# One transformer layer on one core: the column widths of the products in three projection halves

## The chip, the core and the metric

The kernel runs on one core of a Trainium2 chip. The metric is the device time of one execution in microseconds (us), the median over the runs shown. A core has a matrix engine (TensorE, called PE in the profile, with its weight loads shown apart as PEld), a vector engine (DVE), a scalar engine (ACT), a third elementwise engine (POOL) and a queue engine (SP) that starts most transfers from memory.

## The reference

One layer works on 256 tokens of width 2048, in float32. It is a gated linear attention with its own projections, then a squared-ReLU MLP, with an RMSNorm before each and one at the end:

```
proj = rmsnorm(x, gla_norm) @ w_in            # q, k, v, r and a narrow gate
o    = linear attention over chunks of 64 tokens, from q, k, v and the gate
o    = rmsnorm(o, o_norm) * silu(r)
h    = x + o @ w_out
a    = relu(rmsnorm(h, mlp_norm) @ w_up)
out  = rmsnorm(h + (a * a) @ w_down, final_norm)
```

The change touches the two halves of the projection that makes r (2048 by 2048) and the first half of the projection by w_out (2048 by 2048).

## The kernel before

**Number format.** Every large product is made with operands in the format `F32R`, a shortened float32. To get the digits back, each operand is split in two: a high part, made by an ACT copy into `F32R` (line 127, in the profile `hi<-raw`), and a low part, made by a DVE subtraction of the high part (line 131, `lo<-raw,hi`). A product is then the sum of three: high by high, high by low and low by high. The profile shows the matmul's operands as plain `f32` in either format; which format it is follows from the tiles. Plain float32 products are used in a few places, among them the attention scores (line 518, `qt` and `kab`) and the transposes by the identity (line 592).

**A projection half.** `natural` (line 178) computes 256 tokens by 1024 output columns. The tokens are two groups `t` of 128, the 1024 columns are two accumulator banks of 512 (`HALF`), so four banks of PSUM hold the half. The 2048 inner elements are sixteen steps of 128. For each step, `weights` (line 144) allots one of five pairs of weight slots (`wpool`, tags `hi` and `lo`), starts the transfer of 128 by 1024 weights on SP's queue (line 168) and splits them. Then for each `t`, each of the three terms and each bank, `halves` (line 171) issues the products: the stationary operand is 128 by 128 of the activations, the moving operand is the weights. So a step has 2 x 3 x 2 = 12 pairs of stationary operand and bank.

**halves before.** A call covers one bank's 512 columns of one term. It cuts them into pieces of `T` = 256 columns and issues one matmul for each piece:

```
        for c in range(0, n, T) if n % T == 0 else (0,):
            m = slice(c, c + T) if n % T == 0 else slice(0, n)
            nc.tensor.matmul(o[:, m], x, w[:, m], start=first and c == 0, stop=last, skip_group_check=True)
```

A step thus has 24 matmuls of 256 columns, and a half has 384. Every matmul has a weight load of its own in the trace, also where the matmul ahead of it has the same stationary operand. `halves` is also called by the attention (line 561) and by the end of the kernel (line 1089).

**The three halves.** Line 600 makes the first half of r, line 625 the second half, line 646 the first half of the projection by w_out. A fourth call of the same form (line 655) makes the second half of w_out. The sixteen steps take the inner blocks in an order that `even_at` writes out: in the first half step 4 is block 3, in the other two step 4 is block 6; steps 8, 12 and 14 are blocks 8, 12 and 14 in all three. In the second half, block 6 takes its first 128 tokens from a copy in another tile (`xe_gt`).

**Other work on TensorE.** Behind each step but the last, `pump` (line 96) issues one item of a list of side work, in program order among the matmuls: the attention of one head and one token group in the first half, groups of eight 128 by 128 transposes in the other two, at steps 1 and 3. ACT and DVE run ahead of TensorE on the weights as far as the five slots allow.

**The first stage.** The call at line 388 uses cuts of 512, 256 and 272 columns. At its start TensorE waits for the first weights.

Of the kernel before, what the change touches and what calls it, by code (L numbers as in the profile page):

```python
# [32 lines left out]
P = 128  # L33
T = 256
NT = T // P
D = 2048
KT = D // P
# [3 lines left out]
KEYW = HEADS * DK  # L41
# [5 lines left out]
G = 1024  # L47
# [13 lines left out]
EVEN = (5, 6)  # L61
# [7 lines left out]
def tile_gla_mlp(ctx, tc, x, xt, cols, w_vg, w_in, w_gate, w_out, w_up, w_down, final_norm, out):  # L69
    nc = tc.nc  # L70
# [14 lines left out]
    def acc_banks(n):  # L85
        acc_free.rotate(-n)
        return [psum_bank(acc_free[k - n]) for k in range(n)]

    def aux_bank():
        aux_free.rotate(-1)  # L90
        return psum_bank(aux_free[-1], "aux")
# [4 lines left out]
    def pump(n=1):  # L96

        with tc.issue_after(last_hi[0].ins), tc.issue_after(last_lo[0].ins):
            for _ in range(n):
                if side:  # L100
                    side.popleft()()

    def flush():
        while side:
            side.popleft()()
# [38 lines left out]
    def weights(src, n, pieces=None, room=None, gap=None):  # L144


        to = room or slots()
        raw = raw_tile()
        loads, pieces = pieces or ([(0, n)], [(0, n)])
        for s in (slice(*p) for p in loads):  # L150
            dst = raw[:, s]
            if len(src.shape) == 3:
                dst = dst.rearrange("p (i c) -> p i c", i=2)
                with ExitStack() as order:

                    if n_raw[0] == 7:
                        order.enter_context(tc.issue_after(last_load[0].ins))
                    last_load[0] = nc.sync.dma_start(out=dst, in_=src)
                between = SLOT - OFF - 2 * GT if gap else 0
                to = [a[:, OFF - between : OFF + 2 * GT + between].rearrange("p (i c) -> p i c", i=2)[:, :, between:] for a in to]  # L160
                copy_hi(to[0], dst)
                with ExitStack() as order:
                    if last_sum[0]:
                        order.enter_context(tc.issue_after(last_sum[0]))
                    last_lo[0] = nc.vector.tensor_tensor(to[1], dst, to[0].bitcast(F32), op=ALU.subtract)  # L165
                return to
            else:
                last_load[0] = nc.sync.dma_start(out=dst, in_=src[:, s])
        return parts(raw, n, to, pieces)

    def halves(o, x, w, first, last):

        n = w.shape[-1]
        for c in range(0, n, T) if n % T == 0 else (0,):
            m = slice(c, c + T) if n % T == 0 else slice(0, n)
            nc.tensor.matmul(o[:, m], x, w[:, m], start=first and c == 0, stop=last, skip_group_check=True)  # L176

    def natural(row, source, n, cuts, pumps=1, ahead=None, order=range(KT)):

        acc = acc_banks(NT * len(cuts))  # L180
        acc = [acc[t * len(cuts) : (t + 1) * len(cuts)] for t in range(NT)]
        for step, kt in enumerate(order):
            wh, wl = weights(source(kt), n, ahead and ahead(kt))
            terms = lambda t: [(row(kt, t)[x], (wh, wl)[y]) for x, y in ((0, 0), (0, 1), (1, 0))]
            if ahead and step == 0:
                for c, (lo, hi) in enumerate(cuts):
                    for i in (0, 2, 1):
                        for t in range(NT):
                            s, w = terms(t)[i]
                            halves(acc[t][c], s, w[:, lo:hi], i == 0, False)  # L190
            else:
                for t in range(NT):
                    for i, (s, w) in enumerate(terms(t)):
                        for c, (lo, hi) in enumerate(cuts):
                            halves(acc[t][c], s, w[:, lo:hi], step == 0 and i == 0, step == KT - 1 and i == 2)
            if step < KT - 1:
                pump(pumps)
        return acc
# [4 lines left out]
    def turned(row, w, c0, even=(0,), acc=None):  # L203

        acc = acc or acc_banks(GT // P // 2)
        for kp in range(KT // 2):
            wh, wl = pair_of(w, kp, c0, even)
            for i in range(2):
                kt = 2 * kp + i
                ah, al = row(kt)  # L210
                for j in range(GT // P):
                    s = slice(j * P, (j + 1) * P)
                    o = acc[j // 2][:, j % 2 * T : (j % 2 + 1) * T]
                    for n, (u, m) in enumerate(((wh, ah), (wh, al), (wl, ah))):

                        nc.tensor.matmul(  # L216
                            o, u[:, i, s], m, start=kt == 0 and n == 0 and j % 2 == 0,
                            stop=kt == KT - 1 and n == 2, skip_group_check=True,
                        )
                if kt < KT - 1:  # L220
                    pump()
        return acc

    HALF = [(0, 512), (512, 1024)]

    def even_at(a, b):

        order = [kt for kt in range(KT) if kt not in EVEN]
        order.insert(a, EVEN[0])
        order.insert(b, EVEN[1])  # L230
        return order

    def rows(w, c0, n=G, r0=0):
        return lambda kt: w[r0 + kt * P : r0 + (kt + 1) * P, c0 : c0 + n]
# [64 lines left out]
    cuts = [(0, 512), (512, 768), (768, WMAX)]  # L299
# [81 lines left out]
    def put_v(bank, n, t, c0):  # L381
# [4 lines left out]
        )  # L386

    acc = natural(plain_x, rows(w_vg, 0, WMAX), WMAX, cuts, ahead=input_tile)
    flush()
    wrap_input(1, 0, KT - CUT)  # L390
# [90 lines left out]
    for half in range(2):  # L481
        acc = turned(stream_x, w_in, KEYW + half * GT, even=(0,) if half else (2, 3), acc=None if half else [aux_bank(), aux_bank()])
# [18 lines left out]
    for half in range(2):  # L501
        acc = turned(stream_x, w_in, half * GT, even=())
# [39 lines left out]


    acc = natural(row_x, rows(w_in, 3 * KEYW), G, HALF, order=even_at(9, 11))
    flush()
    for t in range(NT):
# [6 lines left out]
    def attend(hd, t):  # L553
        o = aux_bank()
        blocks = [(0, 0)] if t == 0 else [(0, P), (1, T)]
        vs = slice(hd * DV, (hd + 1) * DV)
        n = 0
        for src, lo in blocks:
            a_h, a_l = (a[hd][:, lo : lo + P] for a in (ath, atl))
            for s, v in ((a_h, vh), (a_h, vl), (a_l, vh)):  # L560
                halves(o, s, v[:, src, vs], n == 0, n == 3 * len(blocks) - 1)
                n += 1
        ss = st.tile([P, 1], F32, tag="oss", name="oss")
        sq = tmp.tile([P, DV], F32, tag="t512", name="sq", bufs=1)
        nc.scalar.activation(sq, o, AF.Square, scale=r1k[:, t : t + 1], accum_out=ss)
        nc.vector.tensor_scalar(ss, ss, 1.0 / DV, EPS, op0=ALU.mult, op1=ALU.add)
        rs = st.tile([P, 1], F32, tag="ors", name="ors")
        rsqrt(rs, ss)
        nc.vector.tensor_scalar(on[:, t, vs], o, r1k[:, t : t + 1], rs, op0=ALU.mult, op1=ALU.mult)
# [16 lines left out]
    def turn(src, row, gain, q):  # L586
# [6 lines left out]
        for i in range(4):  # L593
# [3 lines left out]
            nc.scalar.activation(dh, s, AF.Copy, scale=gain(kt))  # L597
            nc.vector.scalar_tensor_tensor(dl, s, gain(kt), dh.bitcast(F32), op0=ALU.mult, op1=ALU.subtract)

    acc = natural(lambda kt, t: (plain_x if kt == EVEN[1] else row_x)(kt, t), rows(w_in, 4 * KEYW), G, HALF, order=even_at(0, 6))  # L600
    flush()
    gate_out(acc, 0)
    oth, otl = (big.tile([P, KT * T + 192], F32R, tag="B", name="ot" + i) for i in "hl")
# [17 lines left out]
    def turns(src, row, gain, q0):  # L621
        return [f for q in (q0, q0 + 1) for f in (nothing, lambda q=q: turn(src, row, gain, q))]

    side.extend(turns(on, turned_o, gain_o, 0))
    acc = natural(row_x, rows(w_in, 5 * KEYW), G, HALF, order=even_at(2, 4))
    flush()
    gate_out(acc, G)

# [14 lines left out]
                sq = tmp.tile([P, 512], F32, tag="t512", name="sq", bufs=1)  # L643
                nc.scalar.activation(sq, h[:, t, lo : lo + 512], AF.Square, accum_out=hs[:, t, lo // 512 : lo // 512 + 1])

    acc = natural(row_o, rows(w_out, 0), G, HALF, order=even_at(2, 4))
    flush()
    add_h(acc, 0)
    hth, htl = (big.tile([P, KT, T], F32R, tag="A" + i, name="h" + i, bufs=1) for i in "hl")
# [5 lines left out]
    acc = natural(row_o, rows(w_out, G), G, HALF, order=even_at(2, 4))  # L655
# [221 lines left out]
    cuts = [HALF, [(0, 512), (512, 768), (768, 1024)]]  # L877
    acc = [[], []]
# [214 lines left out]
    for kt in range(KL):  # L1093
        k = kt - KL + ROOM
        w = weights(rows(w_down, G, G, (ROUNDS - 1) * MR)(kt), G, room=k >= 0 and [room[:, i, k, :] for i in range(2)])
# [20 lines left out]
    for t in range(NT):  # L1116
        for c, (lo, hi) in enumerate(cuts[t]):
            for kt, w in held:
                last_step(kt, w, t, c)
            o = acc[t][c]  # L1120
# [9 lines left out]
            last = nc.vector.tensor_scalar(sf, fs[:, t, n_fs[t] - 1 : n_fs[t]], 1.0 / D, some, op0=ALU.mult, op1=ALU.add)  # L1130
# [5 lines left out]
        for on_act, lo, hi in ((0, 0, 256), (1, 1280, 1536), (0, 256, 768), (1, 1536, 2048), (0, 768, 1280)):  # L1136
            s = hf[:, t, lo:hi]
# [44 lines left out]
```

## Time and profile before

| What | Value |
|---|---|
| Median of the runs | 1048.57 us (1048.22 to 1048.91, 2 runs) |
| Span of the profiled execution, first to last instruction | 1046.7 us |
| First half of r on the span | 190.32 to 242.07 us |
| Second half of r | 242.07 to 287.50 us |
| First half of w_out | 287.50 to 332.93 us |
| TensorE busy, share of the span | 99% |
| DVE busy | 81% |
| ACT busy | 67% |
| Granted TensorE clock, mean | 0.998 |

The profiled execution's own time beside its span is the first row: the runs' median is 1.9 us longer than the span, which is the time ahead of the first instruction and behind the last. A row of the timeline gives the start in us from the span's beginning, the length in us of the merged instructions, the engine, the source line, the operation, the tiles written and read, the shape and the count. A row of the groups ends in the busy time and the mean of one instruction in ns. The length of a matmul in the trace holds the time in which it passes through the array, so consecutive matmuls overlap: what one costs in a stream is read from the distance between starts. A row of the table by stretches gives the stretch, its length, the busy time of each engine with its count of instructions, the granted clock, the busy share of the transfer engines and what they moved.

### The profile page before, as it was taken

The page shows a single profiled execution, that of the slowest core. Times are in us where ns is not written, and L with a number is a line of the kernel's source. Part 1 is how long each engine was busy: PE and PEld are TensorE (multiplying, and loading weights), DVE is VectorE, ACT ScalarE, POOL GpSimd, SP SyncE. Part 2 cuts the span into 40 slices and gives each one's busy share as a digit, 9 for nine tenths or more (in the row PEclk, how much of TensorE's full clock was granted, in tenths as well). Part 3 has the DMA queues.
Part 4 walks back from the last instruction along what each step waited for, and adds up shares of the span by engine and source line. Part 5 has one row for each costly group of instructions (what it writes and reads, how often), then busy time and mean ns, then how long its engine had stood idle before and what let it go on. Part 6 is the DMA issues. An engine that isn't in the chain of part 4 may idle for free. (4 is left out here: it accounts for less than half of the span.)

```text
span 1046.7 us, 23145 instructions
## 1 busy us (share of the span) xinstructions
PE 1038.2 (99%) x9094; PEld 1037.8 (99%) x9094; DVE 843.9 (81%) x1225; ACT 704.2 (67%) x1045; POOL 110.1 (11%) x151
## 2 busy tenths in 40 slices
PE   9999999999999999999999999999999999999997
PEld 9999999999999999999999999999999999999997
DVE  6668645656465566889999999999999999999887
ACT  6785444546455455678678678778778777777785
POOL 0000000010000001111121111121111111211100
PEclk9999999999999999999999999999999999999999
DMA  9957665556655676678888887888888888887772
GB/s 341 332 166 220 188 197 167 156 146 180 199 180 183 187 215 191 169 222 226 227 237 231 238 239 212 247 231 226 237 236 226 238 241 223 234 232 221 236 241 88
DMA packets 112718, 225.21 MB, mean 215 GB/s; under 512 B 10289, under 2 KB 25265, under 8 KB 112481
## 3 DMA queue, kind: packets, MB, share of 16 engines
q1 hardware_dynamic: 95808, 207.39, 64.1%
q0 software_dynamic: 16128, 14.69, 9.3%
q10 hardware_dynamic: 672, 1.66, 0.4%
q8 instruction: 71, 1.16, 0.4%
q14 instruction: 39, 0.31, 0.1%
HBM read 221.60 MB, written 2.10 MB: 214 GB/s over the span
## 5 line engine op out<-in xcount | busy, mean ns | idle before, releaser
L118 ACT CAST hi<-raw 128x768 fp32r<-128x768 f32 (+4 forms) x610 | 490.3, 846 | 281.5 <-PE acc L176 105.5
L131 DVE TENSOR_TENSOR lo<-raw,hi 128x768 fp32r<-128x768 f32 (+3 forms) x226 | 241.8, 1071 | 124.8 <-ACT hi L118 122.2
L720 PE MATMUL acc<-hi,act 128*128 128x256 f32 x1696 | 247.8, 276 | 0.0
L720 PE MATMUL up<-hh,hi 128*128 128x256 f32 x1024 | 238.9, 276 | 0.0
L720 PE MATMUL up<-hl,hi 128*128 128x256 f32 x1024 | 238.8, 276 | 0.0
L165 DVE TENSOR_TENSOR lo<-raw,hi 128x1024 fp32r<-128x1024 f32 x160 | 194.7, 1219 | 30.9 <-ACT hi L118 30.6
L720 PEld LDWEIGHTS acc<-hi,act 128*128 128x128 f32 x1696 | 217.7, 188 | 0.0
L720 PEld LDWEIGHTS up<-hh,hi 128*128 128x128 f32 x1024 | 192.3, 188 | 0.0
L720 PEld LDWEIGHTS up<-hl,hi 128*128 128x128 f32 x1024 | 192.3, 188 | 0.0
L935 POOL DMA_DIRECT2D raw<-in_w_down x112 | 98.4, 878 | 515.0 <-DMA raw<-in_w_down 235.0
L999 DVE TENSOR_TENSOR lo<-raw,hi 128x1024 fp32r<-128x1024 f32 x112 | 136.4, 1218 | 1.6 <-ACT hi L118 1.1
L720 PE MATMUL up<-hh,lo 128*128 128x256 f32 x1024 | 137.0, 276 | 0.0
L720 PE MATMUL acc<-lo,act 128*128 128x256 f32 x848 | 134.0, 276 | 0.0
L720 PEld LDWEIGHTS up<-hh,lo 128*128 128x128 f32 x1024 | 125.7, 188 | 0.0
L720 PEld LDWEIGHTS acc<-lo,act 128*128 128x128 f32 x848 | 113.4, 188 | 0.0
L176 PE MATMUL acc<-hi,xA 128*128 128x256 f32 (+1 forms) x728 | 102.6, 279 | 0.0
L176 PEld LDWEIGHTS acc<-hi,xA 128*128 128x128 f32 x728 | 92.6, 189 | 0.2 <-ACT hi L118 0.2
L176 PE MATMUL acc<-lo,xA 128*128 128x256 f32 (+1 forms) x364 | 57.5, 278 | 0.0
L958 DVE TENSOR_TENSOR raw<-raw 128x256 f32<-128x256 f32 x112 | 47.4, 423 | 2.9
L959 DVE TENSOR_TENSOR raw<-raw 128x256 f32<-128x256 f32 x112 | 47.4, 423 | 2.8
L216 PE MATMUL acc<-xA,hi 128*128 128x256 f32 x288 | 49.2, 276 | 0.0
L176 PEld LDWEIGHTS acc<-lo,xA 128*128 128x128 f32 x364 | 48.9, 188 | 0.0
(159 smaller groups left out, 1197.7 us busy)
## 6 DMA issues: line engine op xcount, KB each, us to landing
raw<-in_w_up SPq DMA_DIRECT2D x128, 512.0 KB, 4.4
raw<-in_w_down SPq DMA_DIRECT2D x224, 256.0 KB, 4.4
raw<-in_w_in SPq DMA_DIRECT2D x80, 512.0 KB, 3.7
raw<-in_w_out SPq DMA_DIRECT2D x32, 512.0 KB, 3.7
raw<-in_w_down POOLq DMA_DIRECT2D x112, 128.0 KB, 5.1
raw<-in_w_down SPq DMA_DIRECT2D x16, 512.0 KB, 4.8
raw<-in_w_vg SPq DMA_DIRECT2D x14, 520.0 KB, 9.1
h<-in_x SPq DMA_DIRECT2D x4, 512.0 KB, 7.5
```

Source lines behind the costliest of these rows:

```text
L118: last_hi[0] = nc.scalar.copy(to, raw)
L131: last_lo[0] = nc.vector.tensor_tensor(lo[:, s], raw[:, s], hi[:, s].bitcast(F32), op=ALU.subtract)
L165: last_lo[0] = nc.vector.tensor_tensor(to[1], dst, to[0].bitcast(F32), op=ALU.subtract)
L176: nc.tensor.matmul(o[:, m], x, w[:, m], start=first and c == 0, stop=last, skip_group_check=True)
L216: nc.tensor.matmul(o, u[:, i, s], m, start=kt == 0 and n == 0 and j % 2 == 0, stop=kt == KT - 1 and n == 2, skip_group_check=True,)
L720: newest[0] = nc.tensor.matmul(o, x, w, start=first, stop=last, skip_group_check=True).ins
L935: nc.gpsimd.dma_start(out=raw[:, :T], in_=src[:, 0, T:], accum_op=ALU.add)
L958: tt(u[:, 2], u[:, 0], u[:, 2], op=ALU.add)
L959: tt(u[:, 1], u[:, 2], u[:, 1], op=ALU.subtract)
L999: last_lo[0] = nc.vector.tensor_tensor(to[1][:, :G], u, to[0][:, :G].bitcast(F32), op=ALU.subtract)
```

## The change

`halves` gets a list of widths. Where a list is given, one call's 512 columns are cut by it; where none is given, the pieces are the ones of before. A table `WIDE` gives the list for four steps, and `natural` looks a step up in it. The three calls named above hand the table over; the fourth half and all other calls of `natural` and `halves` don't.

```diff
-    def halves(o, x, w, first, last):
+    def halves(o, x, w, first, last, widths=None):
 
         n = w.shape[-1]
-        for c in range(0, n, T) if n % T == 0 else (0,):
-            m = slice(c, c + T) if n % T == 0 else slice(0, n)
-            nc.tensor.matmul(o[:, m], x, w[:, m], start=first and c == 0, stop=last, skip_group_check=True)
-
-    def natural(row, source, n, cuts, pumps=1, ahead=None, order=range(KT)):
+        lo = 0
+        for d in widths or ([T] * (n // T) if n % T == 0 else [n]):
+            m = slice(lo, lo + d)
+            nc.tensor.matmul(o[:, m], x, w[:, m], start=first and lo == 0, stop=last, skip_group_check=True)
+            lo += d
+
+    WIDE = {4: [512], 8: [P] * 4, 12: [384, P], 14: [512]}
+
+    def natural(row, source, n, cuts, pumps=1, ahead=None, order=range(KT), wide={}):
...
-                            halves(acc[t][c], s, w[:, lo:hi], step == 0 and i == 0, step == KT - 1 and i == 2)
+                            halves(acc[t][c], s, w[:, lo:hi], step == 0 and i == 0, step == KT - 1 and i == 2, wide.get(step))
...
-    acc = natural(lambda kt, t: (plain_x if kt == EVEN[1] else row_x)(kt, t), rows(w_in, 4 * KEYW), G, HALF, order=even_at(0, 6))
+    acc = natural(lambda kt, t: (plain_x if kt == EVEN[1] else row_x)(kt, t), rows(w_in, 4 * KEYW), G, HALF, order=even_at(0, 6), wide=WIDE)
...
-    acc = natural(row_x, rows(w_in, 5 * KEYW), G, HALF, order=even_at(2, 4))
+    acc = natural(row_x, rows(w_in, 5 * KEYW), G, HALF, order=even_at(2, 4), wide=WIDE)
...
-    acc = natural(row_o, rows(w_out, 0), G, HALF, order=even_at(2, 4))
+    acc = natural(row_o, rows(w_out, 0), G, HALF, order=even_at(2, 4), wide=WIDE)
```

With `P` = 128, steps 4 and 14 have 12 matmuls of 512 columns instead of 24 of 256; step 8 has 48 of 128; step 12 has 12 of 384 and 12 of 128. Over the four steps that is 96 matmuls, as before. No transfer, split, wait or accumulator bank is moved.

## Prediction

> **What bounds the kernel now.** I read the page's head and its slices first, to see which engine sets the time, and then the table by stretches for the changed halves.
>
> ```profile
> span 1046.7 us, 23145 instructions
> PE 1038.2 (99%) x9094; PEld 1037.8 (99%) x9094; DVE 843.9 (81%) x1225; ACT 704.2 (67%) x1045; POOL 110.1 (11%) x151
> ```
>
> TensorE is busy for 99% of the span, and it has as many weight loads (PEld) as matmuls. The head alone doesn't prove that TensorE is the bound, since a matmul's length holds its passage through the array. The stretches do: here are four ordinary steps of the second half (its steps 8 to 11), then that whole half, then the first half of w_out.
>
> ```profile
> core 0: us, PE busy (x) PEld busy (x) DVE busy (x) ACT busy (x) POOL busy (x), PEclk, DMA share, GB/s
> 265.74:276.62 10.88, 10.88 (x99) 10.88 (x97) 4.90 (x4) 4.20 (x4) 0.00 (x0) 1.00 0.60 193
> 242.07:287.50 45.43, 45.43 (x403) 45.43 (x401) 25.55 (x29) 23.37 (x31) 0.00 (x0) 1.00 0.61 186
> 287.50:332.93 45.43, 45.43 (x403) 45.43 (x402) 25.29 (x29) 21.14 (x26) 0.00 (x0) 1.00 0.61 186
> ```
>
> Four steps are 96 matmuls (the other three counted are overlaps at the edges), so a 256-column product costs 10.88 / 96 = 0.1133 us from start to start, and a step of 24 costs 2.72 us. The clock is fully granted, and DVE and ACT are busy for about half of each stretch. Who waits in the two whole halves (242.07 to 332.93 us) is in the table of waits:
>
> ```profile
> ACT hi L118 <- PE acc L176: 40.5, 25, 1.7
> DVE lo L131 <- ACT hi L118: 37.3, 29, 1.5
> ```
>
> ACT, which splits the weights, waits 25 times for TensorE's products to free a slot, and no row has TensorE waiting. So in these halves a microsecond more on TensorE is a microsecond more in the end, and there is no idle time on TensorE that could hide it.
>
> **What sets the 0.1133 us.** A 256-column product is 256 columns of streaming and one weight load, and the load for the next product runs beside the streaming. Which of the two is longer decides what 128 columns cost. Between streaming products the trace can't separate them, but once, at the start of the first stage, TensorE ran dry and the load stands alone. Four timeline rows, each pair from narrow windows on weight loads and on matmuls:
>
> ```profile
> 8.87 0.30 PEld L176 LDWEIGHTS acc<-hi,xA 128*128 128x128 f32 x2 [0.25 <-ACT hi L118]
> 8.98 0.19 PEld L176 LDWEIGHTS acc<-hi,xA 128*128 128x128 f32 x1
> ...
> 8.87 0.39 PE L176 MATMUL acc<-hi,xA 128*128 128x256 f32 x1
> 9.10 0.40 PE L176 MATMUL acc<-hi,xA 128*128 128x272 f32 x2
> ```
>
> The load at 8.87 follows an idle wait. The matmul that needs it is noted at the same moment but is 0.39 us long, 0.11 more than the usual 276 ns: it stood waiting for its weights. The second load starts only at 8.98, 0.11 us after the first, and the second matmul at 9.10. I read this as: a load takes 0.11 us, and the next begins when the product ahead of it begins. Then no product, however narrow, can follow another in less than about 0.11 us.
>
> **What other widths cost.** No row has this format under 256 columns, and the only wider pieces, of 272, stand in the first stage. The nearest rows for the slope are the plain float32 products of the scores:
>
> ```profile
> 164.64 1.70 PE L518 MATMUL aux<-qt,kab 128*128 128x128 f32 x12
> 165.08 0.49 PE L518 MATMUL aux<-qt,kab 128*128 128x192 f32 x2
> 165.41 0.60 PE L518 MATMUL aux<-qt,kab 128*128 128x192 f32 x3
> ...
> L518 PE MATMUL aux<-qt,kab x48: 270/275/328, 164.6 to 187.4; 128*128 128x128 f32 x32, 128*128 128x192 f32 x16
> ```
>
> The first head's first four records are of 128 columns: 165.08 - 164.64 = 0.44, so 0.11 us each. The next two are of 192: 165.41 - 165.08 = 0.33, so 0.165 each. The extra 64 columns cost some 0.055 us, or 0.86 ns a column, about twice the 0.1133 / 256 = 0.44 ns of the changed format, and the code's 24 products are 48 records. So a plain float32 record passes its columns at half speed, and there are two of them for a product. A 192-column record streams like 384 columns of our format: 0.165 us, which is my price for 384. For 512 I add 128 columns at 0.43 ns: 0.165 + 0.055 = 0.22 us.
>
> Bounds for 512: at least 0.215, which is 0.22 less the rounding of rows given to 0.01 us, since no stream in these rows passes a column faster; at most two 256-column products, 0.227, if the excess over pure streaming repeats every 256 columns. For 384 the same: 0.161 to 0.170. Dearer ends come from the lengths of 272 and 256 columns:
>
> ```profile
> L176 PE MATMUL acc<-hi,xA 128*128 128x272 f32 x48 | 13.3, 287 | 0.0
> L176 PE MATMUL acc<-hi,act 128*128 128x256 f32 x96 | 15.6, 276 | 0.0
> ```
>
> 16 columns more are 11 ns, 0.69 ns a column; at that slope 512 would cost 0.113 + 256 x 0.69 ns = 0.29 us. I take 0.22, as the float32 rows give a distance between starts and these only lengths.
>
> Bounds for 128 columns: half of a 256-column product, 0.057 us, if only streaming counted; two plain float32 records, 0.22 us, if narrow pieces lost the fast format. I take 0.1133, the full distance of a 256-column product, because the load row (0.11) is nearest: it is the same operation with the same 128 by 128 operand. There is also a smaller doubt: some products stand 0.12 apart.
>
> ```profile
> 248.87 0.64 PE L176 MATMUL acc<-lo,xe_gt 128*128 128x256 f32 x4
> 249.34 0.64 PE L176 MATMUL acc<-hi,xe_gt 128*128 128x256 f32 x4
> 249.83 0.39 PE L176 MATMUL acc<-hi,xA 128*128 128x256 f32 x2
> ```
>
> From 248.87 to 249.83 are eight products of the copied tile: 0.12 each instead of 0.1133. If narrow pieces all met such a delay, step 8 would cost 48 x 0.12 = 5.76 us.
>
> **A rule against these rows.** The Trainium skill, page "TensorE: Matmul & The Clock Gate", section "Back-to-back issue gap", gives the warm distance of products as N / 2.4 + 2.5 ns, with no term for the weight load: 56 ns at 128 columns. By it the sum below would be near -1 us instead of +9; the same section's sustained 81 ns at 128 columns with loads would give about +4. The trace's 0.1133 at 256 columns stands near that formula's 109, so it can't refute it there, while the load that took 0.11 us alone speaks against both figures at 128.
>
> **The change part by part.** Per half:
> - Step 8: 24 x 0.1133 = 2.72 becomes 48 x 0.1133 = 5.44, so +2.72 us. Half of the array's time goes to waiting for weights.
> - Step 12: 12 x 0.165 + 12 x 0.1133 = 1.98 + 1.36 = 3.34, so +0.62 us. Here the load for the narrow piece is hidden behind 384 columns, and the load for the next 384 behind only 128.
> - Steps 4 and 14: 12 x 0.22 = 2.64 each, so -0.08 twice, -0.16 us. In the second half step 4 has twelve products from the copied tile at 0.12, which could save a little more; I put that at nothing.
> - The issue of instructions: 96 matmuls and 96 loads before and after, nothing.
> - ACT, DVE and the queues: nothing is added. While step 8 is longer, ACT fills its slots and waits for TensorE 2.72 us longer than in the row above; nobody is behind it, because DVE's split waits for ACT's. SP's transfers, issued when a raw buffer frees, come later by the same amount. After the 512-column steps TensorE asks for weights 0.08 us earlier; the cover is ACT's waits of up to 1.7 us, and if that were gone, the step would cost 2.72 as before. POOL has nothing in these halves.
> - The calls without a list issue the same pieces as before: nothing.
>
> The sum per half is 2.72 + 0.62 - 0.16 = +3.18, over three halves +9.5 us. Against the profiled span that is 1046.7 + 9.5 = 1056.2; the runs' median stands 1.9 above the span, so I forecast 1048.57 + 9.5 = 1058 us. Own range: with 0.12 for narrow pieces, +0.40 per half; with the cheapest 384 and 512, about -0.2 per half; so 1057 to 1060, and 1055 to 1062 with rounding in the prices.
>
> **Rivals.**
> - *Narrow pieces lose the fast format* (slower by over 2%). If under 256 columns a product were done as plain float32, it would cost two records, 0.22 us. Step 8: 48 x 0.22 = 10.56, +7.84. Step 12: 1.98 + 2.64 = 4.62, +1.90. Less 0.16: +9.58 per half, +28.7 in all, 1077 us. For it: no piece of this format in the rows is narrower than 256, and the 16 gate columns of the first stage are joined to 256 rather than cut off. Against it: the operands' type, not the width, makes the difference between one and two records in every row.
> - *The load is not the limit* (not slower). A load might overlap the product ahead of it by more than the dry start shows, above all as eight products in a row have the same stationary operand in step 8. It decides from the point where loads can follow each other in 0.057 us. Step 8 is then 48 x 0.057 = 2.74, +0.02; step 12 is 1.98 + 0.68 = 2.66, -0.06; less 0.16: -0.2 per half, -0.6 in all, 1048 us. Against it: the second load at 8.98 waited for the first, and loads are repeated for equal operands already now. The skill's formula above would make this the outcome.
> - *Wide pieces don't stream at the fast rate.* At 0.29 for 512 and 0.20 for 384, steps 4 and 14 take 0.76 us more each in place of 0.08 less, and step 12 rises by a further 0.42: +5.3 per half with the load-bound price of 128, +16 in all, 1064 us. If they streamed at the half speed of a plain float32 record, 0.44 and 0.33, it is 2.72 + 2.60 + 2 x 2.56 = +10.4 per half, +31 in all, 1080 us. Against it: 272 columns cost little more than 256.
> - *The pieces are merged or cut again* on the way to the chip, so that the trace still has 256s: 1048.6 us. Nothing in the rows speaks for it; 272 columns arrive as written.
>
> **How the numbers follow.** My forecast of load-bound narrow pieces has a chance of 0.58; the lost fast format 0.25; the load that is no limit 0.08, with the merged pieces 0.02; wide pieces at the slower slope 0.04, at half speed 0.03. The time is that of the likeliest, 1058. To leave no more than 2 in 10 out, the range has to take in the lost fast format at 1077 with the doubt in its price, so it goes from 1052 to 1080. 2% of 1048.57 is 21 us, and about that is what a measurement of this kernel can tell from no change. My own case lies within it, as do the load that is no limit, the merged pieces and the milder case of the wide ones: 0.71 with a little off for doubt in the sizes. Slower by over 2% are the lost fast format and wide pieces at half speed: 0.28. For faster by 2% nothing speaks: 0.01.
>
> **What would show it.** In the changed profile, the timeline of each half's step 8 should have 48 products 0.11 apart, 5.4 us in all; 0.06 or 0.22 apart decides for a rival. Step 12 should take 3.3 us and steps 4 and 14 some 2.6. TensorE's count should stay 9094; under the lost format some 180 products could turn into twice the records. The fourth half and the MLP should keep their lengths. The prediction is wrong if a narrow piece costs anything but a load, or if TensorE idles in one of these halves.

## The result, and the profile after

The changed kernel takes 1060.68 us (1060.45 to 1060.92, 2 runs) against 1048.57: a ratio of 1.0115, 95% interval 1.0086 to 1.0144, or 12.1 us more. The profiled execution's span went from 1046.7 to 1059.2 us.

The page's head of the changed kernel:

```profile
span 1059.2 us, 23145 instructions
PE 1050.5 (99%) x9094; PEld 1046.8 (99%) x9094; DVE 844.0 (80%) x1225; ACT 704.4 (67%) x1045; POOL 110.1 (10%) x151
```

The counts are those of before, so no narrow product became two records and none was merged or cut. TensorE's busy time grew by 12.3 us, that of DVE and ACT by 0.2 us at most. The table by stretches, with the three changed halves whole:

```profile
core 0: us, PE busy (x) PEld busy (x) DVE busy (x) ACT busy (x) POOL busy (x), PEclk, DMA share, GB/s
190.34:246.11 55.77, 55.77 (x459) 54.77 (x458) 29.30 (x38) 25.69 (x38) 4.39 (x8) 1.00 0.52 150
246.11:295.65 49.54, 49.54 (x403) 48.52 (x402) 25.67 (x29) 23.35 (x31) 0.00 (x0) 1.00 0.57 170
295.65:345.19 49.54, 49.54 (x402) 48.52 (x401) 25.23 (x29) 21.11 (x26) 0.00 (x0) 1.00 0.55 171
```

The second and third half went from 45.43 to 49.54 us, +4.11 each, the first from 51.75 to 55.77. The clock stayed fully granted and TensorE stayed busy. The waits in the second and third half:

```profile
ACT hi L118 <- PE acc L177: 48.6, 25, 4.3
```

ACT waits for TensorE's slots as often as before, for 8.1 us longer in sum (40.5 before): the two halves' extra time on TensorE, nearly. The starts of products in the second half (timeline, TensorE only) give the prices. First step 8, in pieces of 128:

```profile
270.80 1.06 PE L177 MATMUL acc<-lo,xA 128*128 128x128 f32 x8
271.69 1.95 PE L177 MATMUL acc<-hi,xA 128*128 128x128 f32 x16
273.48 1.06 PE L177 MATMUL acc<-lo,xA 128*128 128x128 f32 x8
```

Eight products in 0.89 us, sixteen in 1.79: 0.111 us for 128 columns. Then a piece of step 12, of step 14, and of the ordinary step 15:

```profile
284.89 1.31 PE L177 MATMUL acc<-hi,xE 128*128 128x384 f32 x8
286.03 0.74 PE L177 MATMUL acc<-lo,xE 128*128 128x384 f32 x4
...
290.53 0.62 PE L177 MATMUL acc<-lo,xE 128*128 128x512 f32 x2
290.99 1.07 PE L177 MATMUL acc<-hi,xE 128*128 128x512 f32 x4
...
293.76 1.10 PE L177 MATMUL acc<-hi,xE 128*128 128x256 f32 x8
294.70 0.63 PE L177 MATMUL acc<-lo,xE 128*128 128x256 f32 x4
```

In step 12 a row merges 384s and 128s: four pairs take 286.03 - 284.89 = 1.14 us, 0.285 a pair. Two 512s take 0.46, 0.23 each. The last rows hold the surprise: eight ordinary 256s take 294.70 - 293.76 = 0.94 us, 0.1175 each, where before an ordinary step's products took 0.1133. The two steps between steps 9 and 12 show the same:

```profile
264.52:269.96 5.44, 5.44 (x51) 5.44 (x49) 2.45 (x2) 2.10 (x2) 0.00 (x0) 1.00 0.61 184
278.14:283.80 5.66, 5.66 (x51) 5.66 (x50) 2.45 (x2) 2.10 (x2) 0.00 (x0) 1.00 0.65 185
```

The first row is steps 6 and 7, 2.72 us each; the second is steps 10 and 11, 2.83 each, with the same 48 unchanged products and the same work on ACT and DVE. I call the two paces the fast and the slow rhythm. From the first starts of each step, with the transposes behind step 1 left out, the second half adds up as follows:

| Second half, us | Before | After | Difference |
|---|---|---|---|
| Step 8 (128) | 2.72 | 5.31 | +2.59 |
| Step 12 (384 and 128) | 2.72 | 3.39 | +0.67 |
| Steps 4 and 14 (512) | 2.88, 2.72 | 2.86, 2.76 | +0.02 |
| Steps 9, 10, 11, 13, 15 (unchanged) | 13.60 | 14.24 | +0.64 |
| Steps 0, 1 (unchanged, carried over from the half ahead) | 5.44 | 5.65 | +0.21 |

The sum is +4.13, against the +4.11 of the stretch; each of the other steps changed by 0.01 us at most. The fourth half, unchanged, begins with two slow steps too (+0.21), and from its step 2 on is as before. In the second, third and fourth half step 2 is block 5, with its activations at a shifted address: in the second half its first 128 tokens come from the copied tile (`xe_gt`), and in the other two the block has a place of its own among the blocks of its tile (`place_o` in the code).

The profile of before holds both paces too. In the half ahead of the changed ones, where the attention scores are the side work, 24 ordinary 256s take 2.72 us behind a block from the copied tile, and 2.83 us behind the next head's scores:

```profile
175.92:178.64 2.72, 2.72 (x27) 2.72 (x25) 1.51 (x2) 1.05 (x1) 0.00 (x0) 1.00 0.46 164
181.59:184.42 2.83, 2.83 (x26) 2.83 (x25) 0.92 (x4) 1.67 (x3) 0.00 (x0) 1.00 0.63 185
```

### The profile page after: what moved, and what is told of

It reads as the page before. It is cut to its first block, busy times and chain, and to the rows that moved or that the text cites. A ratio compares the mean times of both kernels' runs of the same rounds, so it can differ in the third digit from the quotient of the medians.

```text
span 1059.2 us, 23145 instructions
## 1 busy us (share of the span) xinstructions
PE 1050.5 (99%) x9094; PEld 1046.8 (99%) x9094; DVE 844.0 (80%) x1225; ACT 704.4 (67%) x1045; POOL 110.1 (10%) x151
## 5 line engine op out<-in xcount | busy, mean ns | idle before, releaser
L177 PE MATMUL acc<-hi,xA 128*128 128x256 f32 (+2 forms) x748 | 106.3, 281 | 0.3 <-ACT hi L118 0.2
L177 PEld LDWEIGHTS acc<-hi,xA 128*128 128x128 f32 x748 | 95.4, 188 | 1.3 <-ACT hi L118 0.7
L177 PE MATMUL acc<-lo,xA 128*128 128x256 f32 (+2 forms) x374 | 59.5, 280 | 0.0
```

Source lines behind the costliest of these rows:

```text
L177: nc.tensor.matmul(o[:, m], x, w[:, m], start=first and lo == 0, stop=last, skip_group_check=True)
```

## The experiments

Each differs from the changed kernel, if nothing else is said, in the table of widths alone; the line of the table that goes out is the same each time and is shown only in the first. Every ratio is against the kernel before.

**Only 512s.**

```diff
-    WIDE = {4: [512], 8: [P] * 4, 12: [384, P], 14: [512]}
+    WIDE = {s: [512] for s in range(KT)}
```

> All sixteen steps of the three halves in pieces of 512 columns. Theory of the load floor and the rhythm: a product costs its columns at 0.443 ns each plus some 2.5 ns, or a weight load of 0.111 us, whichever is longer, and only a product shorter than a load breaks the fast rhythm of 0.1133 us for the 256s. So a 512 costs 0.229 us as in the changed kernel's steps 4, an ordinary step 2.747 in place of 2.720, the blocks from the copied tile save a little, and the fourth half starts at 2.72 a step: about +1.1 us, 1049.7. Rival, any width but 256 breaks the rhythm: the fourth half's steps 0 and 1 take 2.83. Rival of the prediction, 0.22 a product: -3.5 us, 1045.

Measured 1049.85 us against 1048.40, ratio 1.0014 (1.0005 to 1.0023). Nine steps of the second half and then the fourth half's first:

```profile
263.39:288.11 24.72, 24.72 (x110) 20.28 (x109) 1.00 0.62 189
333.83:336.55 2.72, 2.72 (x25) 2.71 (x24) 1.00 0.43 128
```

108 products in 24.72 us are 0.229 each, 2 ns more than two 256s, though the weight loads are busy for only 82% of the stretch: with half the loads there is nothing to win. The fourth half starts in the fast rhythm, so 512 columns don't break it. Fewer, wider products are a small loss.

**Only step 8, in 128s.**

```diff
+    WIDE = {8: [P] * 4}
```

> Only step 8 is changed, in pieces of 128. Load floor and rhythm: step 8 takes 5.31 us (+2.59), and steps 9 to 15 of the half and 0 and 1 of the next stay at 2.83 in place of 2.72, another +0.95 or so; over three halves +10.6, about 1059.2. Rival, the slower steps behind come from the other engines' splits and transfers having been shifted: they fade out within a step or two, as the splits catch up, and the whole is about +8 to +8.5, 1057.

Measured 1059.36 us, ratio 1.0104 (1.0090 to 1.0118). The second half's step 8 and its steps 10 to 15:

```profile
269.61:274.92 5.31, 5.31 (x50) 5.31 (x49) 1.23 (x1) 1.05 (x1) 0.00 (x0) 1.00 0.65 186
277.80:294.76 16.96, 16.96 (x147) 16.96 (x145) 7.68 (x7) 7.59 (x9) 0.00 (x0) 1.00 0.63 187
```

Six unchanged steps take 16.96 us, 2.827 each, with no sign of fading. Step 8 costs 2.59 and the steps behind it about 1.0 a half. A passing shift of the splits is out.

**Only step 12, in 384 and 128.**

```diff
+    WIDE = {12: [384, P]}
```

> Only step 12 is changed, 384 and 128. Load floor and rhythm: step 12 takes some 3.35 us (+0.63 to +0.67), steps 13 to 15 and the next half's 0 and 1 take 2.83, another +0.55; over three halves +3.6, about 1052.2. Rival, shifted splits and transfers: so small a delay shifts little, the steps behind take 2.72, in all +2.0, 1050.6.

Measured 1052.43 us against 1048.40, ratio 1.0038 (1.0025 to 1.0052). Step 12 took 3.38 us in this kernel, and steps 14 and 15 behind it 5.66, slow again. The +4.0 us are a little above the +3.6 expected.

**Step 8 in 64s: is the floor the load?**

```diff
+    WIDE = {8: [P // 2] * 8}
```

> Only step 8 is changed, in 96 pieces of 64. Load floor: each product still costs one load, 96 x 0.111 = 10.6 us for the step (+7.9), with the slow steps behind it +8.9 a half, +26.6 in all, 1075. Rival, narrow pieces stream at half speed (0.86 ns a column, as plain float32 records do) and 128 columns at 0.111 are that: 64 columns cost 0.055, the step 5.3 as with 128, 1059.

Measured 1097.72 us, ratio 1.0468 (1.0449 to 1.0487): neither number. The timeline and the stretches of the second half's step 8 (281.13 to 296.86 us) say why:

```profile
282.84 1.95 PE L177 MATMUL acc<-lo,xA 128*128 128x64 f32 x16
284.62 5.59 PE L177 MATMUL acc<-hi,xA 128*128 128x64 f32 x32
```

```profile
281.13:284.60 3.47, 3.47 (x34) 3.47 (x33) 1.22 (x1) 1.04 (x1) 0.00 (x0) 1.00 0.50 162
281.13:296.86 15.73, 15.73 (x99) 15.73 (x97) 1.22 (x1) 1.04 (x1) 0.00 (x0) 0.66 0.22 71
```

As long as the clock is fully granted, sixteen 64s take 284.62 - 282.84 = 1.78 us, 0.111 each, the price of the 128s. So each product has a floor that doesn't depend on its columns, and streaming at half speed is out. That the floor is the load rests on the dry start, where a load of 0.11 us held back its product; no run here changes the load alone, so another fixed cost of that size for each product isn't excluded. Then the granted clock falls, to a mean of 0.66 over the step, and a product costs 0.213. The expected time had the floor right and didn't foresee the clock.

**Is it the block at a shifted address that brings the fast rhythm back?** Step 8 in 128s, and block 6 moved behind it in the second and third half:

```diff
+    WIDE = {8: [P] * 4}
-    acc = natural(row_x, rows(w_in, 5 * KEYW), G, HALF, order=even_at(2, 4), wide=WIDE)
+    acc = natural(row_x, rows(w_in, 5 * KEYW), G, HALF, order=even_at(2, 9), wide=WIDE)
...
-    acc = natural(row_o, rows(w_out, 0), G, HALF, order=even_at(2, 4), wide=WIDE)
+    acc = natural(row_o, rows(w_out, 0), G, HALF, order=even_at(2, 9), wide=WIDE)
```

> Only step 8 in pieces of 128, and in the second and third changed half block 6, whose activations lie at a shifted address, moves from step 4 to step 9, right behind the narrow pieces. Rhythm restored by the shifted block: steps 10 to 15 and the next half's 0 and 1 take 2.72 in place of 2.83, while steps 4 to 7, now without it behind the transposes, take 2.83; about 1.0 us less than with step 8 alone, 1058.4. Rival, the slow steps come from other engines' shifted work or end only with the half: steps 10 to 15 stay at 2.83, about 1059.8.

Measured 1058.70 us, ratio 1.0097 (1.0083 to 1.0111). The second half's steps 5 to 7, and its steps 10 to 15:

```profile
260.97:269.45 8.48, 8.48 (x74) 8.48 (x73) 4.34 (x5) 3.29 (x4) 0.00 (x0) 1.00 0.59 185
277.60:293.92 16.32, 16.32 (x146) 16.32 (x145) 7.56 (x7) 7.60 (x9) 0.00 (x0) 1.00 0.64 192
```

Steps 10 to 15 are back at 2.72 us, and steps 5 to 7, which lost their block behind the transposes, now take 2.83. Both sides of the expectation came true; the whole is 0.7 us shorter than with step 8 alone, where 1.0 was expected.

**And without any such block.** Step 8 in 128s, and the second half takes all its blocks from the plain place:

```diff
+    WIDE = {8: [P] * 4}
-    acc = natural(row_x, rows(w_in, 5 * KEYW), G, HALF, order=even_at(2, 4), wide=WIDE)
+    acc = natural(plain_x, rows(w_in, 5 * KEYW), G, HALF, order=even_at(2, 4), wide=WIDE)
```

> Only step 8 in pieces of 128, and the second half takes blocks 5 and 6 from their plain place, so it has no block at a shifted address. Rhythm restored by the shifted block alone: the second half's steps 3 to 7 stay at 2.83 in place of 2.72, and the third half recovers at its step 2; about 0.4 us more than with step 8 alone, 1059.8. Rival, the rhythm comes back by itself: steps 3 to 7 take 2.72, and steps 2 and 4 lose the 0.12 us products, 1059.1.

Measured 1060.00 us, ratio 1.0111 (1.0095 to 1.0126). The second half's steps 5 to 7:

```profile
261.42:269.90 8.48, 8.48 (x74) 8.48 (x73) 4.34 (x5) 3.29 (x4) 0.00 (x0) 1.00 0.56 185
```

They take 8.48 us, 2.83 each, against 2.72 with the block at step 2; the third half recovers at its own step 2. The rhythm doesn't come back by itself.

**What breaks it?** My theory at this point was a product shorter than a load. First with 320 and 192:

```diff
+    WIDE = {8: [320, 192]}
```

> Only step 8 is changed, in pieces of 320 and 192 columns. Load floor and rhythm, with any product shorter than a load as the trigger: 320 costs 0.144, 192 a load of 0.111, the step 3.06 (+0.34), and the nine steps behind it 2.83, +0.95: over three halves +3.9, 1052.3. Rival, only pieces of 128 or less break the rhythm: the steps behind take 2.72, +1.0 in all, 1049.4.

Measured 1052.54 us, ratio 1.0038 (1.0025 to 1.0052): step 8 took 3.06 us and the steps 10 to 15 behind it 16.96, slow. That fits the theory, but it also fits any width that isn't a multiple of 256 as the trigger. The next two leave work out so that no product is short: step 8 makes only the first 384, or only the first 272, of each bank's 512 columns.

```diff
+    WIDE = {8: [384]}
```

> Step 8 makes only the first 384 of each bank's 512 columns, in one piece, and leaves the last 128 out, so no product in it is shorter than a load. Trigger is a product shorter than a load: step 8 takes 12 x 0.173 = 2.07 us and the steps behind it 2.72, -1.95 in all, 1046.5. Rival, the trigger is any width that isn't a multiple of 256 (it would also explain why the first stage with its 272s never reaches the fast rhythm): the steps behind take 2.83, +2.9 on top, 1049.4.

```diff
+    WIDE = {8: [272]}
```

> Step 8 makes only the first 272 of each bank's 512 columns, in one piece, and leaves 240 out. Trigger is a product shorter than a load: step 8 takes 12 x 0.123 = 1.48 us and the steps behind 2.72, -3.7 in all, 1044.8. Rival, any width that isn't a multiple of 256: the steps behind take 2.83, 1047.6.

Measured 1049.49 us (ratio 1.0010, 1.0000 to 1.0019) and 1047.82 us (0.9993, 0.9984 to 1.0003), against 1048.57. Step 8 and the seven steps behind it, first with 384, then with 272:

```profile
266.21:268.30 2.09, 2.09 (x15) 2.09 (x14) 0.76 (x1) 1.05 (x1) 0.00 (x0) 1.00 0.66 157
268.30:288.08 19.78, 19.78 (x169) 19.78 (x169) 9.36 (x9) 8.64 (x10) 0.00 (x0) 1.00 0.61 199
```

```profile
265.16:266.67 1.51, 1.51 (x15) 1.51 (x14) 0.18 (x1) 1.05 (x1) 0.00 (x0) 1.00 0.45 138
266.67:286.45 19.78, 19.78 (x170) 19.78 (x169) 9.94 (x9) 8.65 (x10) 0.00 (x0) 1.00 0.65 204
```

Seven steps in 19.78 us are 2.826 each in both kernels. My theory of the trigger fell: products of 384 and 272 columns, all longer than a load, break the rhythm as well. Of the widths tried, 256 and 512 keep it; 64, 128 and 272, 384 by themselves and the pairs of 192 with 320 and of 128 with 384 break it. A kernel that does less work in step 8 thus ends no earlier than before. The first kernel also gives the price of 384 alone: from its first start to the next step's, step 8 takes 2.08 us (2.09 in the row, by rounding), and 2.08 / 12 = 0.173 us.

**Can the finding speed up the kernel before?** Its first stage takes 2.88 us a step. The kernel before, with its blocks 5 and 6 in that stage from the copied tile:

```diff
-    acc = natural(plain_x, rows(w_vg, 0, WMAX), WMAX, cuts, ahead=input_tile)
+    acc = natural(row_x, rows(w_vg, 0, WMAX), WMAX, cuts, ahead=input_tile)
```

> The kernel before, with blocks 5 and 6 of the first stage taken from the copied tile for the first 128 tokens. Rhythm restored by the shifted block, and 272 columns long enough to keep it: steps 7 to 15 take 2.76 in place of 2.88, -1.1 us, 1047.3. Rival, the pieces of 272 disturb the rhythm themselves, or the copy is waited for: no gain, 1048.4 to 1048.8.

Measured 1048.60 us against 1048.47, ratio 1.0001 (0.9992 to 1.0010). Steps 7 to 13 take 20.16 us, 2.88 each, as before. With a piece of 272 in every fourth product, the fast rhythm never sets in; after the two runs above that is what one would expect.

## Why the prediction was right, and what it missed

It forecast 1058 us and 1060.7 was measured. The mechanism of its likeliest case, narrow pieces that each cost a load's time, holds. The nearer range, 1057 to 1060, was just missed; the wider one, 1055 to 1062, held although it had no term for a fifth of the change. The parts that the sum names measure 2.59 + 0.67 + 0.02 = 3.28 us in the second half against 3.18 forecast, and that is so close by luck: 128 columns were priced too dear, 384 and 512 too cheap, and the errors of 0.13, 0.05 and 0.18 us nearly cancel. The sizes, point by point:

- *TensorE is the bound, so its time adds in full.* Right: the halves grew by 12.24 us and the head of the fourth by 0.21, and the span by 12.5.
- *Step 8, a load for each narrow piece: +2.72 forecast, +2.59 measured.* Right. The load's price from the single dry start (0.11) was nearer than the 0.1133 that I put in the sum: 48 x 0.1106 = 5.31. The experiment with 64s shows that the price doesn't hang on the columns, as half of them cost the same at full clock; that it is the load is read from the dry start. The formula of the Trainium skill (page "TensorE: Matmul & The Clock Gate", section "Back-to-back issue gap"), which the page gives for isolated products, would be 56 ns at 128 and 216 at 512, and its sustained figures are 81 and 131; the trace has 111 and 229, so neither holds for this format here.
- *Step 12: +0.62 forecast, +0.67 measured.* The term that was mis-sized is 384 columns: 0.173 us, not the 0.165 read from plain float32 records. 0.173 + 0.111 = 0.284, which is the pair's 0.285.
- *Steps 4 and 14: -0.16 forecast, +0.02 measured in the second half.* The saving had the wrong sign: a 512 costs 0.229, just above the dear end of the range that I had worked out for it (0.227) and not the 0.22 taken. What a 256 costs beyond the rate of the plain float32 records doesn't go away with fewer loads, as I assumed for lack of a row: the run with 512s only has half the loads and gains nothing.
- *"The calls without a list issue the same pieces as before: nothing."* This is the step that failed. The pieces are the same, but ordinary products behind a width that isn't a multiple of 256 cost 0.1178 instead of 0.1133 until a block at a shifted address comes: 0.64 + 0.21 = +0.85 us in the second half, and 12.45 - 3 x 3.28 = 2.6 of the 12.5 us in all. The sign that the fourth half should keep its length failed with it. The profile of before had shown both paces, as the rows of the half ahead do; I quoted the 0.12 us products of the copied tile only as a doubt about narrow pieces, and not the steps of 2.83 behind the scores or of 2.88 in the stage with the 272s.
- *The rivals.* The lost fast format (0.22 for 128 columns), the load that is no limit (0.057) and the slow wide pieces (0.29 for 512) are refuted by the prices above; the merged pieces by the shapes in the rows.

What stays open is why the rhythm depends on the width and on the operand's address. It was only shown what breaks and what restores it; where in the memory or the array the 4.5 ns arise wasn't tried. That it is the address of the restoring block is read from the code: the runs move the block or put it back in its plain place, and none changes an address alone.

## What to carry to other kernels

With a stationary operand of 128 by 128 in this format, price a product at its columns or at one load of 0.111 us, whichever is longer, and get the load from a place where TensorE ran dry. Look in the trace of before for two paces of the same instruction: a change can cost more behind itself than inside, so compare the unchanged steps after a changed one. 256 columns were as good as 512 here, and every other width tried was worse.

## What the hardware did that I had not expected

The slow rhythm: 0.1178 instead of 0.1133 us for an unchanged 256-column product, 4% of the rate. Behind step 8 alone in 128s it lasted nine steps (9 to 15, and 0 and 1 of the next half), some 25 us, with no wait of TensorE in the profile, set by the width of a product long gone.

The clock: with 64 columns a product, TensorE was busy without a gap in the profile, and yet its granted clock fell. In the second half of that run the pace changed from 0.111 to 0.213 us at 286.2 us, 5.1 us after the narrow step began, and back at 299.8, 2.9 us after the 256s had come again. In the first and third half it fell 5.8 and 5.7 us after the narrow step began, and in all three it stayed at 0.50 for 13.7 us. With 128 columns it stayed at 1.00, but a step of those lasts only 5.3 us, so no run shows what a longer stretch would do. The Trainium skill (page "TensorE: Matmul & The Clock Gate", section "Part 1: The HAM clock gate") describes a gate that goes by how busy the array has lately been, and goes to half speed after a window of idle time; here products followed one another without a gap. A thinly used array seems to have been enough, but no run sets this apart from other causes.
